# The small products of the recurrence's inverse, emitted in portions of sixteen columns of blocks

## The chip, the core and the metric

The kernel runs on one core of one Trainium2 chip. A core has a matrix engine (TensorE, PE in the profile, with its weight loads as PEld), three engines for element-wise work (VectorE or DVE, ScalarE or ACT, GpSimd or POOL) and a queue that issues transfers (SyncE, SP). Each engine takes its own instructions in order; between engines semaphores say when data is there. The metric is the device time of one execution in microseconds (us): less is better.

## What is computed

The reference is a two-layer encoder trunk for 256 positions of width 1024. Each layer has a token-mixing part and a channel mixer (dense in layer 0, eight experts in layer 1). Token mixing has two branches, which come out of one input projection and are merged by gates:

```python
for l in range(DEPTH):
    shift, scale, gate = ada_modulation(c, ada_w[l, 0], ada_b[l, 0])
    h = rmsnorm(x, norm_mix[l]) * (1.0 + scale) + shift
    proj = h @ w_in[l]
    ...
    y_a = rwkv7_branch(p_r, p_k, p_v, p_w, p_a, p_g, ...)
    y_b = mla_branch(q_a, kv_a, k_rope, cos, sin, ...)
    merged = jax.nn.sigmoid(g_a) * y_a + jax.nn.sigmoid(g_b) * y_b
    x = x + gate * (merged @ w_o[l])
```

The first branch is a recurrence over the positions, in each of eight heads, on a state of 64 x 64:

```python
def _rwkv7_step(state, inp):
    r, w, k, v, a, b = inp
    sa = jnp.einsum('bhvk,bhk->bhv', state, a)
    state = state * w[:, :, None, :] + sa[..., None] * b[:, :, None, :] + v[..., None] * k[:, :, None, :]
    y = jnp.einsum('bhvk,bhk->bhv', state, r)
    return state, y
```

The kernel computes it in chunks of 64 positions. Inside a chunk the effect of earlier positions on later ones is a triangular system, and its solution needs the inverse of a 64 x 64 triangular matrix for each head and chunk. That inverse is what the change is about.

## The kernel before

**Stages.** The kernel runs, one after the other: token mixing of layer 0 (`mix(0)`), a dense channel mixer (`ffn`), token mixing of layer 1 (`mix(1)`) and the experts (`moe`). A dense product is computed in three parts (L348, L349, L350 in `mm3`): activations and weights are each split into a high part in a faster number format and a remainder. The splits of the weights are an ACT copy (wh, L342) and a DVE subtraction (wl, L343) for each piece of 512 columns; `Stream.take` makes them up to four pieces ahead of use.

**What sets the order in token mixing.** `mix` merges four generators into one program. `dense` goes through a list: projections (a step is 12 products of 128 x 256), and between them products of the conditioning vector on DVE (`ada`, L383, 128 x 1024 each). Three chains run beside it: `rwkv` (the recurrence), `beside` (its side products) and `attend` (the second branch). Each `yield x` of a chain says how much dense work should pass before the chain's next piece: the chain becomes due at the present count plus x times a pace from the table `PACE`, and `mix` emits a chain's piece when it is due, and else a dense step (1.31 on this count for 12 products). A yield of any positive size therefore lets at least one dense step pass. At the entry `?y` of its list, `dense` waits until `rwkv` has reported "y"; `mix` then emits what is left of the recurrence without dense steps in between, and the output projection of the recurrence (`ro`, which reads yhi and ylo) comes next.

**The inverse.** The 64 x 64 triangle is inverted in blocks. DVE makes the inverses of 16 x 16 blocks (L1060 and on), and two levels of small products on PE put them together to 32 x 32 and to 64 x 64. At the first level four products of 32 x 32 stand side by side on the array, one for each of four places (p, d), and 16 columns of blocks (i = 0, 32, ..., 480) follow one another:
- Y0 (L1081, 64 products, the tile is called Y in the profile), then DVE adds the unit matrix and writes Ys (L1083, shown as f, Y, cst).
- M0T (L1090, 32 products) from Ys; DVE copies it (L1093).
- M0 (L1097, 64 products, tile M) from Ys; ACT copies it to AM in four pieces (L1100).
- The second level: Y1 (L1107, 32 products), and T21 (L1116, tile T, 32 products).

Each of these products is two matmul records and two weight loads in the profile (128 of each for Y0). Between the last `yield` of Y0 (1.2) and that of M0 nothing else is emitted on the chain: M0T and M0 follow one another at once.

**The end of the recurrence.** For each half of the positions, the products X, U, S and yps (L1139 to L1179) end in yps; then ACT squares it (ysq), DVE sums and takes a reciprocal root in small steps (yss, L358 to L364) and scales (yn, L1194); PE transposes (yT, L1199), DVE finishes (yo, L1202 and L1204), ACT and DVE split the result into yhi and ylo, which `ro` reads.

Of the kernel before, what the change touches and what calls it, by code (L numbers as in the profile page):

```python
# [322 lines left out]
class K:  # L323
# [571 lines left out]
    def rwkv(self, l):  # L895
# [183 lines left out]
        for i in range(0, 512, 32):  # L1079
            for p, d, q in blocks:  # L1080
                pe.matmul(ps[q:q + 32, i:i + 32], Uo[q:q + 32, i:i + 32], DT[q:q + 32, i:i + 32],  # L1081
                          start=True, stop=True, tile_position=(q, q))
        v.tensor_add(Ys.rearrange("p (c t) -> p c t", c=16), ps.rearrange("p (c t) -> p c t", c=16),  # L1083
                     self.c("eye32").unsqueeze(1).to_broadcast([128, 16, 32]))
        yield 1.2
# [5 lines left out]
                          start=True, stop=True, tile_position=(q, q))  # L1091
        for p, d, q in blocks[::2]:
            v.tensor_copy(DY[q:q + 32].rearrange("p h s -> p (h s)"), p2[q:q + 32])  # L1093
        ps = self.pr_("M0")
        for i in range(0, 512, 32):
            for p, d, q in blocks:
                pe.matmul(ps[q:q + 32, i:i + 32], Ys[q:q + 32, i:i + 32], Dd[q:q + 32, i:i + 32],  # L1097
                          start=True, stop=True, tile_position=(q, q))
        for p, d, q in blocks:
            act.activation(AM[q:q + 32, p, :, 0, 32 * d:32 * d + 32], ps[q:q + 32].rearrange("p (c t) -> p c t", c=16), AF.Copy)  # L1100
        yield 1.2
# [1075 lines left out]
```

## Time and profile before

| | us |
|---|---|
| median of three runs | 1722.49 |
| lowest and highest of the three | 1716.01, 1725.24 |
| profiled execution | 1726.71 |
| its span, first to last instruction | 1724.9 |
| PE busy | 1637.2 (95%) |
| DVE busy | 1458.6 (85%) |
| ACT busy | 1124.8 (65%) |

All times in the rows further down are microseconds from the start of the profiled execution's span. A row of the timeline has the start, the length, the engine, the line of the kernel, the operation with the tile it writes and those it reads, the shapes and how many records it joins; in brackets at its end stands how long the engine was idle before it and whose work ended that. The lengths of PE's records overlap, since products are pipelined: the pace of products is read from one start to the next.

### The profile page before, as it was taken

Reading aid. Unit: us, or ns where it says so; the run is one execution under the profiler, and the core shown is the slowest. Engines: PE = TensorE matmul, PEld = TensorE weight load, DVE = VectorE, ACT = ScalarE, POOL = GpSimd, SP = SyncE. Lnnn points to the kernel's source line nnn. Section 1 sums busy time; section 2 is a strip of 40 time slices with the busy share of each in tenths; the row PEclk is TensorE's granted clock in tenths of the full one; section 3 lists DMA queues with packets and bytes.
Section 4 is the critical chain, followed back from the end, with each engine's and each line's share of the span. In section 5 each row is a group of like instructions: output and inputs, shape, how many; then the busy total and the mean of one; then the engine's idle time right before and its main releaser. Section 6 shows DMA issues by size and latency. Waiting matters only on the chain.

```text
span 1724.9 us, 29083 instructions
## 1 busy us (share of the span) xinstructions
PE 1637.2 (95%) x10976; PEld 1415.8 (82%) x10976; DVE 1458.6 (85%) x2072; ACT 1124.8 (65%) x1481; POOL 6.6 (0%) x19
## 2 busy tenths in 40 slices
PE   4888999999989899989999999999999999999997
PEld 4877999999989789978877778867888678888885
DVE  6887678888868968769889988899898899888985
ACT  3655546555555545557768877778777688667774
POOL 0000000000000000000000000000000000000000
PEclk9998999999989989989999999999999999999998
DMA  8725466888733556778979999989999899999980
GB/s 272 267 91 163 156 192 213 279 294 292 258 110 114 163 169 202 266 311 319 364 293 367 420 420 378 341 329 420 419 418 344 330 380 419 420 370 357 352 342 27
DMA packets 92945, 501.94 MB, mean 291 GB/s; under 512 B 11498, under 2 KB 13034, under 8 KB 49788
## 3 DMA queue, kind: packets, MB, share of 16 engines
q1 hardware_dynamic: 91788, 498.54, 77.4%
q8 instruction: 88, 1.44, 0.3%
q10 hardware_dynamic: 720, 1.42, 0.3%
q14 instruction: 61, 0.50, 0.1%
q0 software_dynamic: 288, 0.03, 0.0%
HBM read 498.91 MB, written 1.05 MB: 290 GB/s over the span
## 4 chain that ended last, share of the span: by engine, by line
PE 83%; DVE 9%; issue 3%; ACT 2%; DMA 2%; DVEq 0%; ACTq 0%; SPq 0%
PE ph L349 7%; PE ph L350 7%; PE ph L348 7%; PE pj L348 6%; PE pj L349 5%; PE pj L350 5%; PE py L349 4%; PE py L350 4%; PE ph L1884 3%; PE ph L1883 3%; PE py L348 3%; DVE el L265 3%; PE psh L348 2%; PE psh L349 2%; PE psh L350 2%
## 5 line engine op out<-in xcount | busy, mean ns | idle before, releaser
L265 DVE TENSOR_TENSOR el<-er,eh 128x2048 fp32r<-128x2048 f32 (+1 forms) x268 | 585.8, 2220 | 25.6 <-ACT eh L259 14.7
L259 ACT ACTIVATE eh<-er 128x2048 fp32r<-128x2048 f32 (+1 forms) x268 | 491.1, 1862 | 50.5 <-PE ph L350 17.3
L342 ACT ACTIVATE wh<-wr 128x512 fp32r<-128x512 f32 (+1 forms) x366 | 223.5, 620 | 213.1 <-PE pj L349 65.4
L343 DVE TENSOR_TENSOR wl<-wr,wh 128x512 fp32r<-128x512 f32 (+1 forms) x366 | 243.1, 674 | 66.2 <-ACT wh L342 64.9
L348 PE MATMUL pj<-hhi,wh 128*128 128x256 f32 x704 | 210.0, 303 | 10.9 <-ACT hhi L468 9.9
L350 PE MATMUL pj<-hhi,wl 128*128 128x256 f32 x704 | 203.7, 291 | 0.6 <-DVE wl L343 0.6
L349 PE MATMUL pj<-hlo,wh 128*128 128x256 f32 x704 | 203.8, 291 | 0.1
L348 PEld LDWEIGHTS pj<-hhi,wh 128*128 128x128 f32 x704 | 137.0, 197 | 19.2 <-ACT hhi L468 11.1
L265 DVE TENSOR_TENSOR el<-x,eh 128x2048 fp32r<-128x2048 f32 x66 | 144.0, 2202 | 5.5 <-ACT eh L259 2.6
L349 PEld LDWEIGHTS pj<-hlo,wh 128*128 128x128 f32 x704 | 139.5, 198 | 2.9 <-issue 1.8
L350 PEld LDWEIGHTS pj<-hhi,wl 128*128 128x128 f32 x704 | 139.1, 198 | 1.6 <-DVE wl L343 0.8
L259 ACT ACTIVATE eh<-x 128x2048 fp32r<-128x2048 f32 x66 | 121.1, 1853 | 12.9 <-PE ph L350 5.4
L349 PE MATMUL py<-el,eahi 128*128 128x512 f32 x272 | 108.0, 397 | 3.4 <-DVE el L265 3.3
L350 PE MATMUL py<-eh,ealo 128*128 128x512 f32 x272 | 106.3, 391 | 0.0
L348 PE MATMUL py<-eh,eahi 128*128 128x512 f32 x272 | 101.5, 390 | 0.0
L349 PE MATMUL psh<-xu,wh 128*128 128x258 f32 x336 | 95.3, 284 | 0.0
L348 PE MATMUL psh<-xu,wh 128*128 128x258 f32 x336 | 95.2, 283 | 0.0
L350 PE MATMUL psh<-xu,wl 128*128 128x258 f32 x336 | 94.9, 282 | 0.0
L383 DVE SCALAR_TENSOR_TENSOR wr<-wr,cB 128x1024 f32<-128x1024 f32 x64 | 78.0, 1220 | 19.8 <-DMA wr<-in_ada_w_dram 19.6
L348 PE MATMUL ph<-eh,hhi 128*128 128x512 f32 x224 | 89.9, 404 | 0.0
L349 PE MATMUL ph<-el,hhi 128*128 128x512 f32 x224 | 89.0, 398 | 0.6 <-DVE el L265 0.6
L349 PE MATMUL ph<-el,hlo 128*128 128x512 f32 x224 | 88.6, 396 | 0.0
(469 smaller groups left out, 3642.8 us busy)
## 6 DMA issues: line engine op xcount, KB each, us to landing
er<-in_moe_w_dram SPq DMA_DIRECT2D x268, 1024.0 KB, 7.9
x<-in_moe_w_dram SPq DMA_DIRECT2D x66, 1024.0 KB, 7.6
wr<-in_ada_w_dram SPq DMA_DIRECT2D x64, 512.0 KB, 4.3
wr<-in_w_in_dram SPq DMA_DIRECT2D x52, 512.0 KB, 4.1
wr<-in_ffn_up_dram SPq DMA_DIRECT2D x44, 512.0 KB, 4.5
aw<-in_ada_w_dram SPq DMA_DIRECT2D x32, 512.0 KB, 4.8
wr<-in_ffn_w_dram SPq DMA_DIRECT2D x22, 512.0 KB, 4.5
wr<-in_w_o_dram SPq DMA_DIRECT2D x16, 512.0 KB, 4.3
```

The costliest lines, as they stand in the source:

```text
L259: self.k.tc.keep_in_program_order(nc.scalar.activation(t[4][:, :t[2]], t[3][:, :t[2]], AF.Copy))
L265: nc.vector.tensor_sub(t[5][:, :t[2]], t[3][:, :t[2]], t[4][:, :t[2]].bitcast(F32)))
L342: self.nc.scalar.activation(hi, src, AF.Copy)
L343: self.nc.vector.tensor_sub(lo, src, hi.bitcast(F32))
L348: mm(out, whi, xhi, start=start, stop=False, skip_group_check=True)
L349: mm(out, whi, xlo, start=False, stop=False, skip_group_check=True)
L350: mm(out, wlo, xhi, start=False, stop=stop, skip_group_check=True)
L383: x = v.scalar_tensor_tensor(w, w, 1.0, self.cB, op0=OP.mult, op1=OP.mult, accum_out=mod[:, n:n + 1])
L1883: pe.matmul(ps, x[0], w[0], start=start, stop=False, skip_group_check=True)
L1884: pe.matmul(ps, x[0], w[1], start=False, stop=stop, skip_group_check=True)
```

## The change

Seven `yield 0.1` are added to the recurrence's chain: after each of the first three quarters of Y0's products, between M0T's copies and M0, and after each of the first three quarters of M0's. What is computed, the number of instructions that compute it and their sizes stay as they are. The table `PACE` and the other yields are unchanged.

```diff
@@ -1080,6 +1080,8 @@
             for p, d, q in blocks:
                 pe.matmul(ps[q:q + 32, i:i + 32], Uo[q:q + 32, i:i + 32], DT[q:q + 32, i:i + 32],
                           start=True, stop=True, tile_position=(q, q))
+            if i % 128 == 96 and i < 480:
+                yield 0.1
         v.tensor_add(Ys.rearrange("p (c t) -> p c t", c=16), ps.rearrange("p (c t) -> p c t", c=16),
                      self.c("eye32").unsqueeze(1).to_broadcast([128, 16, 32]))
         yield 1.2
@@ -1091,11 +1093,14 @@
                           start=True, stop=True, tile_position=(q, q))
         for p, d, q in blocks[::2]:
             v.tensor_copy(DY[q:q + 32].rearrange("p h s -> p (h s)"), p2[q:q + 32])
+        yield 0.1
         ps = self.pr_("M0")
         for i in range(0, 512, 32):
             for p, d, q in blocks:
                 pe.matmul(ps[q:q + 32, i:i + 32], Ys[q:q + 32, i:i + 32], Dd[q:q + 32, i:i + 32],
                           start=True, stop=True, tile_position=(q, q))
+            if i % 128 == 96 and i < 480:
+                yield 0.1
         for p, d, q in blocks:
             act.activation(AM[q:q + 32, p, :, 0, 32 * d:32 * d + 32], ps[q:q + 32].rearrange("p (c t) -> p c t", c=16), AF.Copy)
         yield 1.2
```

After the edit a line number behind L1082 is greater by 2 to 5. The rows that follow are the order in which the two kernels give instructions to an engine, without times; rows of "..." leave out products that repeat the ones above them.

On PE, in layer 0, from Y0 (tile Y_1660) to M0, before; `pj<-` are the dense products, `sc` is the attention's:

```order
L1081 MATMUL Y_1660<-f_1262,f_1260 32x32 x64
L349 MATMUL pj<-hlo,wh 128x256
...
L1408 MATMUL sc<-kT_1640,qT_1642 128x128 x2
L1090 MATMUL M0T<-f_1263,f_1262 32x32 x32
L1097 MATMUL M_1788<-f_1262,f_1263 32x32 x64
```

and now, the same place:

```order
L1081 MATMUL Y_1660<-f_1262,f_1260 32x32 x16
L349 MATMUL pj<-hlo,wh 128x256
...
L1081 MATMUL Y_1660<-f_1262,f_1260 32x32 x16
L1413 MATMUL sc<-kT_1640,qT_1642 128x128 x2
...
L1432 MATMUL pT<-cst,e 128x128 x2
L1092 MATMUL M0T<-f_1263,f_1262 32x32 x32
...
L1100 MATMUL M_1894<-f_1262,f_1263 32x32 x16
L1413 MATMUL sc<-kT_1641,qT_1643 128x128 x2
```

Four portions of Y0 and four of M0 now stand where one of each stood. Between the first portion of Y0 and M0T there are 41 dense products in layer 0 (5 before) and 48 in layer 1 (17 before), and between the portions of M0 12 each.

On PE, at the end of the recurrence in layer 0: the last transposes yT and what follows them, before (the output projection, `pj<-yhi`, comes 60 dense products and three groups of the attention further on):

```order
L1437 MATMUL o<-eT,vv 64x128 x4
L1199 MATMUL yT<-cst,yn 128x128 x4
L348 MATMUL pj<-hhi,wh 128x256
L349 MATMUL pj<-hlo,wh 128x256
L350 MATMUL pj<-hhi,wl 128x256
```

and now:

```order
L350 MATMUL pj<-hhi,wl 128x256
L1204 MATMUL yT<-cst,yn 128x128 x4
L348 MATMUL pj<-yhi,wh 128x256 x2
L349 MATMUL pj<-ylo,wh 128x256
L350 MATMUL pj<-yhi,wl 128x256
```

The output projection has moved right behind yT; in layer 1 too, where 72 dense products stood between them. Between yps and yT stand 36 dense products in layer 0 (60 before) and 60 in layer 1 (60 before).

On DVE, the same end in layer 0, from the scaling yn to the split ylo, before:

```order
L1194 TENSOR_TENSOR yn<-yps,rs_y 128x512
...
L1202 SCALAR_TENSOR_TENSOR yo<-yT,prm,pv 128x128 x4
L343 TENSOR_TENSOR wl<-wr,wh 128x512
L1204 TENSOR_TENSOR yo<-yo,gate 128x4x128
L343 TENSOR_TENSOR wl<-wr,wh 128x512
L383 SCALAR_TENSOR_TENSOR wr,mod_1616<-wr,cB 128x1024
L343 TENSOR_TENSOR ylo<-yo,yhi 128x4x128
```

and now:

```order
L364 SCALAR_TENSOR_TENSOR rs_y<-rs_t,rs_y 128x8
L383 SCALAR_TENSOR_TENSOR wr,mod_1616<-wr,cB 128x1024
L1199 TENSOR_TENSOR yn<-yps,rs_y 128x512
L343 TENSOR_TENSOR wl<-wr,wh 128x512
L1207 SCALAR_TENSOR_TENSOR yo<-yT,prm,pv 128x128 x4
L1209 TENSOR_TENSOR yo<-yo,gate 128x4x128
L383 SCALAR_TENSOR_TENSOR wr,mod_1616<-wr,cB 128x1024
L343 TENSOR_TENSOR ylo<-yo,yhi 128x4x128
```

Two splits of weights (wl) have left the chain from yo to ylo, and a product of the conditioning (L383) has come in ahead of yn.

## Rows read from the trace of the kernel before

**Rows 1.** The page: busy time, share and instructions of each engine; the instruction queue.

```profile
PE 1637.2 (95%) x10976; PEld 1415.8 (82%) x10976; DVE 1458.6 (85%) x2072; ACT 1124.8 (65%) x1481; POOL 6.6 (0%) x19
...
q8 instruction: 88, 1.44, 0.3%
```

**Rows 2.** Stages: length; busy us of PE, PEld, DVE, ACT, POOL; clock; DMA; GB/s.

```profile
161.20:167.90 6.70, 6.69 (x116) 5.75 (x116) 2.13 (x5) 2.35 (x4) 0.00 (x0) 0.55 0.54 165
167.90:236.00 68.10, 67.82 (x798) 62.02 (x796) 49.64 (x133) 40.26 (x99) 0.00 (x0) 1.00 0.47 148
604.90:620.90 16.00, 14.87 (x206) 13.29 (x197) 6.35 (x11) 7.94 (x14) 0.00 (x0) 0.50 0.57 185
620.90:693.00 72.10, 71.59 (x756) 66.28 (x755) 59.27 (x155) 40.71 (x103) 0.00 (x0) 1.00 0.60 189
```

**Rows 3.** Timeline of PE in layer 0, M0T and M0.

```profile
154.95 0.66 PE L1090 MATMUL M0T<-f,f 32*32 32x32 f32 x29 [0.60 <-DVE f L1083]
155.84 0.69 PE L1090 MATMUL M0T<-f,f 32*32 32x32 f32 x32 [0.23 <-issue]
...
156.42 0.95 PE L1097 MATMUL M<-f,f 32*32 32x32 f32 x89
161.21 0.74 PE L1097 MATMUL M<-f,f 32*32 32x32 f32 x35 [3.83 <-issue]
```

**Rows 4.** Timeline of PE in layer 1: M0T, M0 and Y1.

```profile
602.43 1.16 PE L1090 MATMUL M0T<-f,f 32*32 32x32 f32 x61 [1.66 <-DVE f L1083]
...
603.46 1.60 PE L1097 MATMUL M<-f,f 32*32 32x32 f32 x126
...
607.98 1.92 PE L1107 MATMUL Y<-f,AM 32*32 32x32 f32 x64 [1.14 <-DVE wr L383]
```

**Rows 5.** Timeline of ACT in layer 1: the four copies of M0.

```profile
605.09 2.39 ACT L1100 ACTIVATE AM<-M 32x512 f32<-32x512 f32 x4 [1.33 <-PE M L1097]
```

**Rows 6.** Transfers from 150 to 170 us: packets, MB, share of 16 engines.

```profile
q8 instruction: 4, 0.07, 1.3%
```

**Rows 7.** Timeline of PE in layer 0: the last yps, and two dense products.

```profile
219.58 1.04 PE L1179 MATMUL yps<-Sb,AR 128*64 128x128 f32 x8
...
231.02 0.28 PE L349 MATMUL pj<-hlo,wh 128*128 128x256 f32 x1
231.14 0.28 PE L350 MATMUL pj<-hhi,wl 128*128 128x256 f32 x1
```

**Rows 8.** Timeline of DVE in layer 0, the end of the recurrence.

```profile
222.51 0.47 DVE L1419 TENSOR_SCALAR e<-e,rsum 128x128 f32<-128x128 f32 x2
...
225.61 0.68 DVE L1194 TENSOR_TENSOR yn<-yps,rs_y 128x512 f32<-128x512 f32 x1
...
231.20 1.12 DVE L1202 SCALAR_TENSOR_TENSOR yo<-yT,prm,pv 128x128 f32<-128x128 f32 x4
232.23 0.68 DVE L343 TENSOR_TENSOR wl<-wr,wh 128x512 fp32r<-128x512 f32 x1
232.83 0.68 DVE L1204 TENSOR_TENSOR yo<-yo,gate 128x512 f32<-128x512 f32 x1
...
234.03 1.22 DVE L383 SCALAR_TENSOR_TENSOR wr<-wr,cB 128x1024 f32<-128x1024 f32 x1
...
235.18 0.69 DVE L343 TENSOR_TENSOR ylo<-yo,yhi 128x512 fp32r<-128x512 f32 x1
```

**Rows 9.** Timeline of DVE in layer 1: Ys.

```profile
601.69 0.68 DVE L1083 TENSOR_TENSOR f<-Y,cst 128x512 f32<-128x512 f32 x1
```

**Rows 10.** Table of stages, at waits in layer 1.

```profile
565.00:569.00 4.00, 2.46 (x24) 2.36 (x25) 3.65 (x14) 2.26 (x7) 0.00 (x0) 1.00 0.45 131
569.00:573.00 4.00, 4.00 (x29) 3.69 (x28) 2.62 (x9) 1.28 (x4) 0.00 (x0) 0.62 0.55 148
584.00:588.00 4.00, 2.97 (x14) 2.09 (x13) 3.96 (x16) 1.76 (x5) 0.00 (x0) 1.00 0.51 140
588.00:592.00 4.00, 3.75 (x30) 3.30 (x29) 3.56 (x9) 3.17 (x8) 0.00 (x0) 1.00 0.39 128
```

## The prediction

> **What bounds the kernel now.** I read the page first: TensorE (PE) is busy 95% of the span [rows 1], so time can only come from the places where it stands still or runs slowly. The table of busy time and granted clock by stage then says which of these belong to the changed lines. From 161.2 to 167.9 us (layer 0) the granted clock is 0.55, nearly all of it at the lower level (1.2 GHz); from 604.9 to 620.9 us (layer 1) it is 0.50 throughout. In the stretches behind each, up to the end of the recurrence, it is 1.00 with PE busy in 67.8 of 68.1 and 71.6 of 72.1 us [rows 2]. So the rest of the mixing stage is bound by PE and whatever is saved ahead of it arrives at its end, unless something new waits there.
>
> The PE timeline shows how the dips begin. In layer 0 the product M0T waits 0.60 us for DVE (Ys), then runs, and M0 stops in its middle for 3.83 us with "issue" as the releaser: no data is awaited [rows 3]. In layer 1 M0T waits 1.66 us for Ys, and Y1 1.14 us (the profile names an unrelated DVE instruction; what Y1 really needs are ScalarE's four copies of M0, 2.39 us [rows 5], which start only when M0 has ended) [rows 4]. The clock is at the lower level after that pause, and after that run of small products with its waits.
>
> What is the pause? The instruction queue moved 88 blocks, 1.44 MB, in the whole run [rows 1], for 21952 PE instructions (10976 products, as many weight loads): about 250 instructions to a block. From 155.84 us to the pause, PE issues 128 small products with their weight loads (121 of them in the two rows, 7 in short rows between), that is 256 instructions in 1.5 us [rows 3]: one block. Four blocks came in the 20 us around it [rows 6], so a block per 5 us is what is seen when PE asks for the most, about 50 instructions per us. I take the pause for the wait for the next block.
>
> **The change part by part: what it gives.** No product is added or removed. Y0 and M0 (256 instructions each) now come in four portions of 64, and a dense step of 12 products stands between most of them: twelve at 0.12 us [rows 7], 1.4 us.
> 1. The pause. A portion and its step are 64 + 24 instructions, with the attention's products some 95, in about 0.3 + 1.4 + 0.4 = 2.1 us: 45 per us against the 50 seen. The pause should go: 3.83 + 0.23 us in layer 0. Whether a short one remains I cannot read from before: 0 to 1 us.
> 2. The waits of M0T. Ys is pushed back on DVE, since two attention steps and two products of the conditioning (L383, 1.15 us each [rows 8]) now stand ahead of it there; but PE has 41 dense products instead of 5 to do in between, 4.9 us. In layer 0 that about covers it: the 0.60 us goes. In layer 1 DVE comes late out of the rotary products (Ys could start at 601.69 us [rows 9]) and now has three splits (0.60 each) and two L383 ahead of Ys, 4.1 us: ready at 606.4 us. PE got to M0T at 602.43 - 1.66 = 600.8 us with 17 dense products behind Y0; with 48 it gets there 31 x 0.12 = 3.7 us later, and about 1.0 for three more breaks and a group of transposes: 605.5. So the 1.66 us becomes about 0.9. Y1's 1.14 us is covered by a dense step and three groups of transposes, 2.5 to 3 us, against the 2.39 us of copies: 0.3 left.
> 3. The clock. With a dense step after every 0.3 us of small products the mixture is like that of the later recurrence, which runs at 1.00 [rows 2]. Of the 6.7 us at 0.55 in layer 0, 0.45 x 6.7 = 3.0 come back; of the 14.87 busy us at 0.50 in layer 1, half: 7.4.
> Layer 0 gives 4.06 + 0.60 + 3.0 = 7.7, layer 1 0.8 + 0.8 + 7.4 = 9.0, together 16.7. Against it I set 1.3 us of new waits of dense products for their split weights: DVE has to make them in a time in which it was busy for only 2.13 of 6.7 and 6.35 of 16.0 us [rows 2], so it has the room, but not always in time (bounds 0 and 4). Gain: 15.4.
>
> **What it costs: the end of the recurrence.** Each of the seven new yields lets a dense step pass, so the recurrence ends seven steps later in the program, while the dense work ahead of "?y" stays the same. Before, 60 dense products stood behind the last yT in layer 0 and 72 in layer 1; now none do, and the first product of the output projection, which reads yhi and ylo, stands right behind yT in both. Nothing hides this chain any more.
> - From yT to ylo: in layer 0 DVE starts yo at 231.20 and ylo at 235.18 us [rows 8]. Two splits (0.60 each) that stood in the chain are gone in the new order, L383 is still there: 235.18 + 0.6 - 231.20 - 1.2 = 3.4 us. Two products that need only yhi (0.24) come earlier. PE idle: 3.2 us, in each layer.
> - Ahead of yT: from the end of yps (219.58 + 1.04) to the end of yn (225.61 + 0.68) before took 5.7 us [rows 7, 8]; the new order drops a softmax piece (0.47) and gains an L383 (1.15): 6.4 us. In layer 0 PE has only 36 dense products and one attention group for it, about 4.9 us: idle 1.5. In layer 1 it keeps 60 products and five groups, over 9 us: 0.
> - L383 stands ahead of both yn and ylo, and may wait for its weights; I add 0.5 us for each layer.
> Sum: 3.2 + 1.5 + 0.5 + 3.2 + 0.5 = 8.9 us.
> - The clock again. An idle PE loses it: with 2.46 us of work in 4.0 (1.54 idle), the next 4.0 us had 0.62 [rows 10]. The tails have less work than that, so I expect it in both layers. Price by that case: 0.38 of 4 us, that is 1.5 us; by layer 0's stretch behind M0, 3.0. I take 2.0 each: 4.0 us.
>
> Sum: -15.4 + 8.9 + 4.0 = -2.5 us. Against the profiled execution's own 1726.71 us that is 1724.2; it lies 4.2 us above the median of the three runs, 1722.49, so the forecast in terms of the median is 1720.0.
>
> **A rule that speaks against it.** The row shows 88 blocks of 16 KB on the instruction queue [rows 1]. The Trainium skill, "Runtime: NRT & Kernel Launch", section "Instruction fetch mechanics", says the same of the blocks (16 KiB, 256 instructions) and that the cost of crossing a block's boundary is mostly hidden. By that rule the 3.83 us would not be the fetch, and spreading the products would not remove it; the third rival below prices this from the rows.
>
> **The rivals.** First, **cheap tails**: no new waits on splits, no L383 that waits, and the clock keeps its level through the tails, because yT and the two early products cut the idle time into pieces. For it: 1.03 us of idle time in 4.0 elsewhere cost nothing in the clock [rows 10]; against it: the tails' pieces are longer. Then -16.7 + 7.9 = -8.8 us: 1713.7, and less where the lead that the splits win during the idle time saves a later wait. Chance 0.25.
> Second, **slower, by layer 1's dense steps starving**: Y0 ended at about 600.8 - 17 x 0.12 = 598.8 us, so PE wants its dense steps from there on, while DVE is in its rotary products until 601.69 us [rows 9]. If the dense products wait there for over some 2 us, PE is left with portions of 0.3 us and idle time, the clock falls as before, and now 36 more dense products lie in the slow stretch at 0.12 us more each, 4.3 us. Layer 1's gain turns to a loss of 4.3, layer 0 gives 7.7, the tails cost 12.9: +9.5 us, 1732.0. Against it: the splits are made up to four pieces ahead of their use. Chance 0.11.
> Third, **the portions don't remove the pause**, since it is not the fetch or comes at the next block. Layer 0 loses its 4.06 and 3.0 us: -2.5 + 7.1 = +4.6, 1727.1. Against it: layer 1 issues the same products (M0's 126 records run through in 1.60 us [rows 4]), so it is not the products themselves. Chance 0.11.
> The forecast has the rest, 0.53.
>
> **How the numbers follow.** Half a per cent, 8.6 us, is about what a measurement of this kernel can tell from no change. The forecast's own range is 1714 to 1727 (pause left over 0 to 1, splits 0 to 4, clock in the tails 0 to 6.0). It lies within the half per cent. Faster by over 0.5% (under 1713.9): 0.15 of the first rival and 0.06 of the forecast, 0.21. Slower (over 1731.1): 0.07 of the second and 0.05 of the others, 0.12. Same: 0.67. The range takes in the first rival and the third, and reaches just to the second's edge: 1711 to 1731.
>
> **What would show it.** Right: no "issue" pause in M0, M0T's wait in layer 1 near 1 us, the clock at 1.00 from 152 to 168 and 597 to 621 us; and, new, PE waiting for yo/yhi/ylo at the output projection's first products, 3 us in each layer, with a lower clock in the 4 us behind it. Wrong: a pause of several us that turns up in another small product; no idle time ahead of the output projection; or a clock of 0.5 among the portions of layer 1. The last would make the change slower, the absence of the tail faster than I say.

## The result: 0.6% slower

The median went from 1718.47 us (11 runs, 1714.19 to 1726.30) to 1729.23 us (11 runs, 1724.87 to 1740.34). The ratio is 1.0061, with a 95% interval of 1.0041 to 1.0080: 10.5 us slower (7.0 to 13.7). The forecast was 1720.0 with 0.12 for "slower by over 0.5%"; the time lies in its range of 1711 to 1731, but on the other side of no change.

The profiled execution after took 1734.05 us (span 1732.3), the one before 1726.71. Both lie above their medians, by 4.8 and 8.2 us, so the difference of the two spans is not the change's. I therefore also took one piece of equal work out of each trace: from the start of the 780th dense product (tile "pj") before the sum of squares "rms" that closes layer 0's mixing stage, up to that sum, and the same from the 800th in layer 1. These two pieces took 143.2 + 163.5 = 306.7 us before and 148.3 + 168.9 = 317.2 us after: 5.1 us more in layer 0 and 5.4 in layer 1. The rest of the program is the same within its own scatter.

The page of the changed kernel, busy time of PE:

```profile
PE 1637.1 (95%) x10976; PEld 1415.1 (82%) x10976; DVE 1461.2 (84%) x2072; ACT 1125.7 (65%) x1481; POOL 6.6 (0%) x19
```

The share is that of [rows 1]: nothing is to be seen there. The table of stages shows it (length; busy us of PE, PEld, DVE, ACT, POOL; granted clock; DMA share; GB/s), the changed kernel:

```profile
151.00:161.80 10.80, 8.66 (x180) 7.81 (x180) 8.74 (x20) 5.77 (x14) 0.00 (x0) 1.00 0.62 191
161.80:170.40 8.60, 8.60 (x169) 7.93 (x170) 7.23 (x15) 3.56 (x10) 0.00 (x0) 0.80 0.62 183
182.50:236.00 53.50, 53.03 (x636) 48.35 (x628) 36.96 (x103) 29.29 (x71) 0.00 (x0) 1.00 0.48 149
236.00:250.00 14.00, 8.23 (x41) 7.70 (x42) 7.51 (x15) 2.51 (x5) 0.00 (x0) 0.63 0.44 149
598.00:608.00 10.00, 8.38 (x181) 7.57 (x180) 8.89 (x16) 3.58 (x7) 0.00 (x0) 1.00 0.89 297
608.00:624.50 16.50, 14.71 (x335) 13.25 (x336) 12.85 (x29) 9.21 (x23) 0.00 (x0) 1.00 0.75 240
624.50:629.00 4.50, 4.50 (x80) 4.28 (x80) 2.18 (x5) 2.40 (x4) 0.00 (x0) 0.62 0.67 219
692.00:700.00 8.00, 6.81 (x31) 6.51 (x32) 4.47 (x9) 1.89 (x3) 0.00 (x0) 0.57 0.33 112
```

Compare with [rows 2]. The small products of layer 1 now run at a clock of 1.00 (598 to 624.5 us), as the change wanted it. But each layer has a dip among or behind the small products (161.8, 624.5) and a new one at the end of the recurrence (236, 692), where PE is busy for 8.23 of 14 and 6.81 of 8 us. Before, these ends stood at 1.00, with 13.27 of 14 us busy in layer 0 and no idle time in layer 1:

```profile
236.00:250.00 14.00, 13.27 (x115) 12.79 (x114) 9.70 (x19) 6.46 (x11) 0.00 (x0) 1.00 0.71 231
692.00:696.00 4.00, 4.00 (x37) 3.73 (x36) 3.12 (x7) 1.75 (x4) 0.00 (x0) 1.00 0.89 277
```

**The end of the recurrence.** The timeline of PE at the last yT and the first products of the output projection, layer 0 and then layer 1 (start, duration, line, tiles; in brackets the idle time before it and what ended it):

```profile
237.34 0.66 PE L1204 MATMUL yT<-cst,yn 128*128 128x128 f32 x4 [1.80 <-DVE yn L1199]
240.59 0.80 PE L348 MATMUL pj<-yhi,wh 128*128 128x256 f32 x2 [2.60 <-ACT yhi L342]
243.22 0.58 PE L349 MATMUL pj<-ylo,wh 128*128 128x256 f32 x1 [1.83 <-DVE ylo L343]
...
244.45 0.41 PE L348 MATMUL pj<-yhi,wh 128*128 128x256 f32 x1
244.66 0.41 PE L349 MATMUL pj<-ylo,wh 128*128 128x256 f32 x1
...
692.90 0.80 PE L348 MATMUL pj<-yhi,wh 128*128 128x256 f32 x2 [2.37 <-ACT yhi L342]
693.99 0.58 PE L349 MATMUL pj<-ylo,wh 128*128 128x256 f32 x1 [0.29 <-DVE ylo L343]
```

6.23 us idle in layer 0 and 2.66 in layer 1, and behind it dense products that start 0.21 us apart instead of 0.12 [rows 7]: 25 of them in layer 0 and 24 in layer 1, some 2.3 us each. Together 13.5 us. Of the last wait in layer 0, the 1.83 us for ylo, most is a conditioning product (L383) ahead of ylo on DVE, which waited 1.45 us for its own weight:

```profile
241.32 1.23 DVE L383 SCALAR_TENSOR_TENSOR wr<-wr,cB 128x1024 f32<-128x1024 f32 x1 [1.45 <-DMA wr<-in_ada_w_dram]
```

**Behind the small products.** Layer 0, PE and then ACT, and the queue that loads the weights (SPq):

```profile
161.78 0.64 PE L1398 MATMUL qkT<-cst,q 128*96 128x128 f32 x4 [2.12 <-ACT e L1420]
...
166.93 0.52 PE L1100 MATMUL M<-f,f 32*32 32x32 f32 x32
...
169.43 0.45 PE L1100 MATMUL M<-f,f 32*32 32x32 f32 x32
```

```profile
160.19 0.63 ACT L342 ACTIVATE wh<-wr 128x512 fp32r<-128x512 f32 x1 [2.45 <-DMA wr<-in_w_in_dram]
160.73 0.46 ACT L1420 ACTIVATE e<-sc,mx 128x256 f32<-128x256 f32 x1
```

```profile
146.47 0.33 SPq L171 DMA_DIRECT2D wr<-in_ada_w_dram  x1
152.97 1.81 SPq L171 DMA_DIRECT2D wr<-in_w_in_dram  x2
```

and the same place before, ACT and the queue:

```profile
157.51 0.63 ACT L342 ACTIVATE wh<-wr 128x512 fp32r<-128x512 f32 x1 [2.97 <-DMA wr<-in_w_in_dram]
```

```profile
147.29 0.33 SPq L171 DMA_DIRECT2D wr<-in_ada_w_dram  x1
153.78 2.08 SPq L171 DMA_DIRECT2D wr<-in_w_in_dram  x2
```

The portions of M0 run without the "issue" pause of [rows 3]. But PE now waits 2.12 us for the exponentials "e" of the attention. They stand in ScalarE's queue behind a weight's split, and that waits 2.45 us for its weight, one of the two loads issued from 152.97 us on; the queue had issued nothing since 146.47 us. The gap in the loads is not new: before it lay between 147.29 and 153.78 us, and ScalarE waited 2.97 us for a weight behind it. What is new is that PE comes to the work behind that split before the weight is there. In layer 1, PE and then DVE:

```profile
608.06 1.20 PE L1092 MATMUL M0T<-f,f 32*32 32x32 f32 x64 [1.67 <-DVE f L1085]
...
620.28 0.64 PE L1398 MATMUL qkT<-cst,q 128*96 128x128 f32 x4 [0.64 <-ACT e L1420]
...
622.85 0.44 PE L1432 MATMUL pT<-cst,e 128*128 128x128 f32 x2 [1.10 <-DVE kT L1404]
```

```profile
606.16 1.23 DVE L383 SCALAR_TENSOR_TENSOR wr<-wr,cB 128x1024 f32<-128x1024 f32 x1 [0.67 <-DMA wr<-in_ada_w_dram]
...
607.32 0.69 DVE L1085 TENSOR_TENSOR f<-Y,cst 128x512 f32<-128x512 f32 x1
```

M0T waits as long as before [rows 4], now because a product of the conditioning, itself late by 0.67 us for its weight, stands ahead of Ys on DVE; and two products of the attention wait for 0.64 and 1.10 us.

**What a portion costs by itself.** PE in layer 1, a dense product, a portion of M0, and the dense products behind it:

```profile
610.59 0.28 PE L350 MATMUL pj<-hhi,wl 128*128 128x256 f32 x1
610.79 0.45 PE L1100 MATMUL M<-f,f 32*32 32x32 f32 x32
611.18 0.38 PE L348 MATMUL pj<-hhi,wh 128*128 128x256 f32 x1
611.40 0.28 PE L349 MATMUL pj<-hlo,wh 128*128 128x256 f32 x1
611.52 0.28 PE L350 MATMUL pj<-hhi,wl 128*128 128x256 f32 x1
```

Starts of dense products lie 0.12 us apart; from the last one to the portion it is 0.20, from the first one behind the portion to the next 0.22. A break therefore costs some 0.18 us, and seven more of them 1.3 us in each layer.

### The profile page after: what moved, and what is told of

Its sections match the earlier page's. It is cut to its first block, busy times and chain, and to the rows that moved or that the text cites. A ratio compares the mean times of both kernels' runs of the same rounds, so it can differ in the third digit from the quotient of the medians.

```text
span 1732.3 us, 29087 instructions
## 1 busy us (share of the span) xinstructions
PE 1637.1 (95%) x10976; PEld 1415.1 (82%) x10976; DVE 1461.2 (84%) x2072; ACT 1125.7 (65%) x1481; POOL 6.6 (0%) x19
## 4 chain that ended last, share of the span: by engine, by line
PE 80%; DVE 10%; DMA 4%; issue 2%; ACT 2%; DVEq 0%; ACTq 0%; SPq 0%
PE ph L349 7%; PE ph L350 7%; PE ph L348 7%; PE pj L348 5%; PE pj L349 5%; PE pj L350 5%; PE py L349 4%; PE ph L1889 3%; PE py L350 3%; PE ph L1888 3%; PE py L348 3%; DVE el L265 3%; PE psh L348 2%; PE psh L349 2%; PE psh L350 2%
## 5 line engine op out<-in xcount | busy, mean ns | idle before, releaser
L383 DVE SCALAR_TENSOR_TENSOR wr<-wr,cB 128x1024 f32<-128x1024 f32 x64 | 78.0, 1222 | 16.9 <-DMA wr<-in_ada_w_dram 16.6
```

Of the source, the lines that this page charges most:

```text
L383: x = v.scalar_tensor_tensor(w, w, 1.0, self.cB, op0=OP.mult, op1=OP.mult, accum_out=mod[:, n:n + 1])
```

## The experiments

Twelve runs, in which a "step" is a dense step of 12 products that is let past, so that the recurrence ends one step later. The column of the mixing stages is the equal work of the section above, from one trace each; us are worked out from the ratio and the median of before (1717 to 1721 us) beside it.

| kernel | steps | ratio to before (95%) | us | mixing stages, us |
|---|---|---|---|---|
| before | 0 | 1 | 0 | 306.7 |
| changed | 7 | 1.0061 (1.0041 to 1.0080) | +10.5 | 317.2 |
| late_seven | 7 | 1.0082 (1.0062 to 1.0102) | +14.1 | 320.8 |
| after_mo_first | 7 | 1.0012 (0.9999 to 1.0026) | +2.1 | 303.0 |
| late_seven_mo | 7 | 1.0017 (1.0001 to 1.0033) | +2.9 | 309.0 |
| before_mo_first | 0 | 1.0002 (0.9987 to 1.0016) | +0.3 | 306.6 |
| m0_two_halves | 1 | 0.9993 (0.9979 to 1.0006) | -1.2 | 300.7 |
| m0_two_halves_again | 1 | 1.0011 (0.9995 to 1.0028) | +1.9 | 307.2 |
| y0_portions_only | 3 | 0.9981 (0.9965 to 0.9996) | -3.3 | 302.3 |
| m0_portions_only | 4 | 0.9963 (0.9948 to 0.9979) | -6.4 | 298.2 |
| m0_portions_mo_first | 4 | 0.9950 (0.9927 to 0.9973) | -8.6 | 297.9 |
| halves_both | 2 | 0.9931 (0.9908 to 0.9954) | -11.9 | 295.5 |
| halves_again | 2 | 0.9935 (0.9912 to 0.9958) | -11.2 | 295.0 |
| halves_mo_first | 2 | 0.9938 (0.9913 to 0.9964) | -10.7 | 292.6 |

Theory A: the loss is the wait at the recurrence's output projection, because the recurrence ends seven steps later. Theory B: the portions themselves cost.

**The delay alone.** late_seven is the kernel before with

```
+        for _ in range(7):
+            yield 0.1
         ps = self.pr_("Y0")
```

> The kernel before, with no portions, but seven dense steps let past ahead of Y0 in one piece, so that the recurrence ends as late as in the changed kernel. Theory A: the tails' cost without the portions' saving: 11 to 16 us above before, idle time of 5 to 6 us and a lower clock at the recurrence's projection in layer 0, 2 to 3 us idle in layer 1. Theory B: within 3 us of before.

Measured: 14.1 us above before (10.7 to 17.5). Its list of PE's waits in layer 0 (us in total, times, longest):

```profile
PE M L1099 <- issue: 4.2, 1, 4.2
PE pj L348 <- ACT yhi L342: 2.6, 1, 2.6
PE pj L349 <- DVE ylo L343: 2.1, 1, 2.1
PE pT L1429 <- ACT e L1417: 2.0, 1, 2.0
PE yT L1201 <- DVE yn L1196: 1.8, 1, 1.8
```

The same three waits at the end as in the changed kernel, without any portion: B, which wanted it within 3 us of before, cannot be the whole. The pause in M0 is there as well (4.2 us), and so is a wait of 2.0 us for "e", without portions and ahead of the pause. The delay also moves the inverse itself: in layer 1 its lower clock lasts from 624.3 to 631.1 us only, where before it stood at 0.50 from 604.9 to 620.9 us [rows 2]. So the 14.1 us are not the tail alone.

**The tail taken away.** after_mo_first and before_mo_first exchange the output projections, which puts the attention's 96 dense products behind the last yT:

```
-        body += ["?y"] + each([f"ro{c}" for c in range(4)])
         body += ["?o"] + each([f"mo{c}" for c in range(4)])
+        body += ["?y"] + each([f"ro{c}" for c in range(4)])
```

> The changed kernel with the two output projections of each layer in the other order (attention's first, the recurrence's second), so that 96 dense products lie behind the last yT. Theory A (the loss is the wait of the recurrence's output projection: in the changed kernel 6.2 us idle and 3.2 us at the lower clock in layer 0, 2.7 and 3.1 us in layer 1, 15.2 together): no idle time over 0.5 us ahead of either projection, clock 1.0 there, and 3 to 5 us below the kernel before (13 to 15 below the changed kernel). Theory B (the portions themselves cost, by breaks in the dense work and new waits on the engines beside; the end of the recurrence only shows a wait that would come elsewhere): within 3 us of the changed kernel, so 7 to 10 us above before.

> The kernel before with the same exchange of the two projections and nothing else. Theory A: nothing to gain, because no wait stood ahead of the recurrence's projection: 0 in layer 0, and in layer 1, where the last product of the attention came 2 us after the projection's start, 0 to 3 us slower. If this alone gains 3 us or more, the exchange has a merit of its own and its run on the changed kernel does not speak for theory A.

Measured: 2.1 us above before (0.2 below to 4.5 above), and for the control 0.3 (2.2 below to 2.7 above). The two tails of after_mo_first in the table of stages:

```profile
236.00:250.00 14.00, 14.00 (x122) 14.00 (x121) 13.79 (x28) 6.61 (x12) 0.00 (x0) 1.00 0.79 249
682.00:690.00 8.00, 8.00 (x69) 7.66 (x69) 7.39 (x16) 3.85 (x9) 0.00 (x0) 1.00 0.58 192
```

PE is full and the clock at 1.00 where the changed kernel had 8.23 of 14 us and 0.63. So the tail is what made the change slower: without it 8.4 us are back, and the exchange has no merit of its own. But both theories are off on the rest. A wanted a gain of 3 to 5 us over before to remain, since the portions were to save something; by the medians none is seen: 2.1 us against 0.3 for the control, with intervals that overlap. By the single traces 3.6 us are seen (303.0 against 306.6).

**What the portions save.** late_seven_mo is late_seven with the same exchange.

> The seven dense steps ahead of Y0 in one piece and no portions, with the attention's output projection ahead of the recurrence's, so that nothing waits at the end of the recurrence. Against the changed kernel with the same exchange (1719.4, 2 us above before) only the portions are missing, so the difference is what the portions themselves save. Theory A (from the two runs with the tail, 1732.7 against 1729.2): they save 3 to 4 us: 4 to 7 us above before. If they save what the prediction's sum said, 15 us: 17 above. If nothing: 2 above.

Measured: 2.9 us above before (0.2 to 5.7), that is 0.9 us above after_mo_first. A saving of 15 us, which would have put it at 17, is excluded. By the traces the difference is 6.0 us (309.0 against 303.0), but the two intervals overlap and a single trace does not carry a few us (next experiment): from nothing to some 6 us is what can be said. It is also a saving over an inverse that the delay had already changed: here, too, the lower clock of layer 1's inverse is left from 617.2 to 620.7 us only, without any portion. What tests the sum's gain of 15.4 is after_mo_first against before_mo_first.

**One yield in M0.** m0_two_halves is the kernel before with

```
                           start=True, stop=True, tile_position=(q, q))
+            if i == 224:
+                yield 0.1
```

in M0 alone.

> The kernel before with one yield in the middle of M0 and no other, one dense step of delay against the 60 and 72 dense products in hand behind the last yT. If the 3.83 us pause in M0 of layer 0 is the fetch of the next block of instructions and one dense step covers it, it is gone: 3 to 5 us below before, or 6 to 7 if the clock behind it comes back too. If the pause only moves to another place among the small products: within 2 us of before.

> M0 alone in two halves, measured again, because its first median (1 us below before) and its trace disagree: there the two mixing stages together are 6 us shorter than in the kernel before (300.7 against 306.7 us), as those of Y0 and M0 in halves are 11 us shorter, which its medians bear out. If the trace is right: 4 to 8 us below before. If the first median is right, the second half, that of Y0, is worth 10 us: 0 to 2 below.

Measured: 1.2 us below before (3.6 below to 1.0 above) and 1.9 above (0.9 below to 4.8 above): no difference, and the 4 to 8 us that the first trace promised are not there. The second halves of M0 in layer 0, of the first and of the second trace:

```profile
156.03 0.61 PE L1097 MATMUL M<-f,f 32*32 32x32 f32 x47 [0.62 <-issue]
```

```profile
157.56 0.64 PE L1097 MATMUL M<-f,f 32*32 32x32 f32 x47 [2.19 <-issue]
```

One step in its middle shortens the pause from 3.83 us [rows 3], to 0.62 in one execution and 2.19 in another, and does not remove it. In layer 1 both traces have a new "issue" pause ahead of a dense product (1.32 and 1.92 us), where the kernel before waited 1.14 us at Y1 [rows 4]. So the pause moves, as the second reading has it. The mixing stages of the two traces differ by 6.5 us, nearly all of it in layer 1 (161.0 and 167.2): a single trace of this kernel does not carry a few us.

**Portions in Y0 or in M0 alone.**

> Portions in Y0 alone: three steps of delay. Theory A with a threshold: in the kernel before, layer 0 had 3.9 us in hand between ylo (235.8) and the first product of the output projection (239.7), 2.7 steps of 1.45 us, and layer 1 some 8.7 us, 6 steps; the three steps cost 0.5 us in layer 0 and nothing in layer 1, the pause in M0 stays: 1 us below to 2 above before. Rival without a threshold (each step costs its share of 14 us in seven): 5 to 6 above.

> Portions in M0 and the yield behind M0T alone: four steps of delay. Theory A with the threshold: layer 0 is over by 1.3 steps, 1.9 us idle and 1 to 3 us at the lower clock, layer 1 by nothing; the pause in M0 is gone, of which some 1 to 3 us arrive: 1 us below to 3 above before. Rival without a threshold: 6 to 8 above, less the pause.

Measured: 3.3 us below before (0.7 to 6.0), and 6.4 below (3.6 to 8.9). Both are better than either expectation. The rival without a threshold falls: three and four steps cost nothing like their share of 14 us. The first products of the projection in layer 0, of y0_portions_only and then m0_portions_only:

```profile
239.06 0.39 PE L348 MATMUL pj<-yhi,wh 128*128 128x256 f32 x1 [0.20 <-ACT gb L764]
240.31 0.39 PE L349 MATMUL pj<-ylo,wh 128*128 128x256 f32 x1 [0.86 <-DVE ylo L343]
```

```profile
233.43 0.50 PE L348 MATMUL pj<-yhi,wh 128*128 128x256 f32 x2 [1.67 <-ACT yhi L342]
235.12 0.39 PE L349 MATMUL pj<-ylo,wh 128*128 128x256 f32 x1 [1.19 <-DVE ylo L343]
```

1.06 us idle at three steps, 2.86 at four, 6.23 (with the wait ahead of yT) at seven; in layer 1 neither has a wait there. With one step of 1.45 us and 2.7 steps in hand in layer 0, a straight line gives 0.4, 1.9 and 6.2. In layer 0 the threshold is there; it is softer than the line. The two traces also tell the other costs apart. PE in y0_portions_only, layer 0 and layer 1:

```profile
165.49 0.64 PE L1395 MATMUL qkT<-cst,q 128*96 128x128 f32 x4 [1.94 <-ACT e L1417]
```

```profile
609.87 0.64 PE L1099 MATMUL M<-f,f 32*32 32x32 f32 x30 [3.60 <-issue]
```

The wait for the late weight by way of "e" comes with the portions of Y0 (1.94 us; 0.63 with those of M0), or rather with the dense steps let past ahead of M0T: late_seven has it without portions. And the pause, which the kernel before had only in layer 0, stands here in layer 1 and not in layer 0: it is no property of one product.

**Two halves each.** halves_both has the yield of m0_two_halves in Y0 and in M0.

> Y0 and M0 in two halves each, one yield in the middle of each: two steps of delay, within what both layers have in hand. Theory A: no wait at the output projection, no pause in M0: 1 to 4 us below before. Rival without a threshold: 2 to 4 above, less the pause.

> The kernel with Y0 and M0 in two halves each, measured again beside before, because its gain of 0.7% came out three times as large as expected. Theory A (threshold at the end of the recurrence, pause gone in layer 0): 6 to 13 us below before if the gain is real; 1 to 4 below if the first measurement was a lucky one.

Measured: 11.9 us below before (7.9 to 15.8), and on another chip 11.2 (7.2 to 15.1); the medians alone are 8.6 and 10.3 us apart. The gain is real; it is far over the 1 to 4 us that I gave it first. Stages of halves_again, both inverses (the kernel before has 0.79 from 151.8 to 168 and 0.77 from 597.2 to 610 us), and its list of PE's waits in layer 0:

```profile
151.30:165.50 14.20, 13.54 (x444) 12.12 (x444) 13.58 (x30) 9.25 (x21) 0.00 (x0) 1.00 0.59 188
585.70:600.70 15.00, 12.18 (x439) 11.18 (x438) 12.35 (x22) 6.57 (x12) 0.00 (x0) 1.00 0.86 278
```

```profile
PE qkT L1397 <- DVE q L1378: 1.0, 1, 1.0
PE pj L349 <- DVE ylo L343: 0.4, 1, 0.4
...
PE M L1099 <- issue: 0.3, 1, 0.3
PE Y L1111 <- issue: 0.3, 1, 0.3
```

The pause is down to 0.3 us, no wait for "e" has come in its place, the clock stays at 1.00 in both inverses, and 0.4 us is all that waits at the projection. In layer 1 a pause of 1.91 us is left in the middle of M0. Of the 11.2 us by the traces (306.7 against halves_both's 295.5), 8.2 are in layer 0.

**The exchange where little waits.**

> The two halves with the attention's output projection ahead of the recurrence's. Theory A: the two steps of delay lie within what is in hand, only 0.4 us was idle at the output projection, so the exchange has nothing to take away: within 3 us of the halves alone. If the end of the recurrence still costs something that the idle time does not show: 3 us or more below them.

> Portions in M0 and the yield behind M0T, with the attention's output projection first. Theory A: four steps are over the threshold of layer 0, where 2.9 us were idle at the output projection; they go, so 2 to 5 us below the same kernel without the exchange, 8 to 12 below before. If the end of the recurrence does not matter at four steps: within 1 us of it.

Measured: 10.7 us below before (6.2 to 15.0), the same as the halves without it; and 8.6 below (4.6 to 12.6), 2.2 under m0_portions_only. The exchange is worth 0 at two steps, some 2 at four, 8 to 11 at seven: as theory A has it, though at four steps the two intervals overlap.

What the runs leave open: why seven steps without a tail (after_mo_first) lie 12.8 us above two (halves_mo_first). Their traces differ by 5.6 us in layer 0 and 4.9 in layer 1. Read from them: in layer 0 a wait of 1.93 us for "e", a clock of 0.77 from 157 to 172 us behind it, and five more breaks of 0.18; in layer 1 waits of 2.05 us ahead of M0T, 0.89 and 0.40 for the attention, and 1.26 in the recurrence, where halves_mo_first has 0.61 ahead of M0T, a pause of 0.90 in M0 and 0.19 for the attention. That the late weights are the cause in layer 0 is argued from the order of ScalarE's queue and was not tried by itself; what the runs show is that the wait is there with three or seven dense steps ahead of M0T, with portions or without, and not with one.

## Why the prediction was wrong, step by step

The sum was -15.4 for the inverse, +8.9 for idle tails, +4.0 for the clock in them: -2.5. The runs put +2.1 in the place of the first term (after_mo_first) and +8.4 in the place of the other two (changed against after_mo_first): +10.5. **The step that failed is the gain of 15.4.** Its mechanisms came, but the new waits that it allowed for (1.3 us), the clock that it counted on in layer 1 (7.4 us) and the breaks that it put at nothing were mis-sized; items 2 to 5 have what they measured.

1. The pause. Right: it is gone from M0 in layer 0, and no other small product has it. Most of the 4.06 us is taken up by a new wait: with three dense steps let past ahead of M0T, PE comes to the gap in the loads earlier and waits 2.12 us for "e", with the clock down for 12 dense products and a portion behind it (some 1.2 us). The removed pause does not bring this wait: late_seven has both, and halves_both neither, and its layer 0 is 8.2 us shorter.
2. The waits ahead of M0T. Layer 0: gone, as forecast. Layer 1: 1.67 instead of 0.9; I had counted the work ahead of Ys on DVE (4.1 us) but not that L383 would wait for its own weight, 0.67. Y1's own wait is gone, but 0.64 and 1.10 stand ahead of it at the attention's products.
3. The clock. The mechanism was right in layer 1: 1.00 all through the small products. Its size was too large. Half of 14.87 us was to come back; at the lower level a dense product takes 0.21 us against 0.12, Y1's 64 took 1.92 [rows 4] against 1.20 after. With 32 dense products in that stretch at 0.09 each, 0.7 us each for Y1 and T, and 1.3 for X, U and the attention's qkT, some 5.6 of the 7.4 us were there to be had. And two new dips, behind the new waits, took part of it back: in layer 0 that of item 1, in layer 1 another 12 dense products, some 1.1 us.
4. The 1.3 us for new waits of dense products (bounds 0 and 4). This is the term that was mis-sized most. I asked whether DVE could make the split weights in time; what was late was the weight itself, on ScalarE's queue, and the attention's work stood behind it. Waits and the dips behind them come to 3.3 us in layer 0, and 1.7 us of waits alone in layer 1.
5. The breaks between small and dense products were costed at nothing. They take 0.18 us each, 2.5 us in all. With 0.8 us from item 2, 1.8 and 1.1 from item 3 and 3.7 from item 4 (3.3 + 1.7, less the 1.3 allowed), some 10 of the 15.4 us are accounted for. The rest, a gain of some 5 us, is near the 3.6 us of the single traces with the exchange (303.0 against 306.6), while their medians show none; that difference stays open.
6. The tails. Idle 6.23 us in layer 0 and 2.66 in layer 1, against 3.2 + 1.5 + 0.5 and 3.2 + 0.5: 8.9 forecast, 8.9 in the trace. That the sum fits is luck: layer 0 is 1.0 us over, mostly because L383 waited 1.45 us for its weight where 0.5 was set, and layer 1 is 1.0 under. The clock behind them, 4.0 forecast, is some 4.6. With the traces' 13.5 us against the forecast's 12.9, the mechanism and its size hold; late_seven's 14.1 agrees, though its delay changed more than the tail. By the exchange only 8.4 come back, in part since the recurrence's projection, now last, makes its own consumers wait (two of 0.7 us at the merged halves in layer 0); the rest of that difference is open.

The rivals. "Cheap tails" falls. "Slower by layer 1's dense steps starving" had the right side for the wrong reason: from 598 to 608 us, where it wanted waits and a low clock, the clock is 1.00. "The portions don't remove the pause" falls for the changed kernel.

What the pause is. Where small products follow each other for long, there are pauses of 3.83 us before, 4.2 in late_seven, 3.60 in y0_portions_only, 0.3 and 1.91 with two halves; there is none over 0.5 us with M0 in four portions, where dense products lie between every 64 of its instructions (the changed kernel, m0_portions_only and both with the exchange). The traces say more: they have the times of the packets on the instruction queue (q8, [rows 1]). Before, one ended at 159.86 us, and PE went on at 161.21, 1.35 us later. The same holds for every "issue" pause of PE of over 0.5 us in the mixing stages of all fourteen traces, 20 pauses in ten of them: each ends 1.2 to 1.5 us behind the end of a block's packet. That the pause is the wait for the next block, as the prediction took it, is what this timing shows; no run changed the fetch itself. The Trainium skill, "Runtime: NRT & Kernel Launch", section "Instruction fetch mechanics", says that the cost of crossing a block's boundary is mostly hidden. The traces agree with that for the portions, and not for the long runs of small products. One reading of the prediction is put in doubt by the same times: Y1's 1.14 us before [rows 4] also ended 1.50 us behind a packet's end (606.48 us), and 0.50 behind the copies that the prediction named, so it may have been a wait for a block too.

The base was too high as well: the three runs shown had a median of 1722.49, eleven have 1718.47. From there the same sum would have given 1716.

The version that beats both is halves_both: 1711.97 and 1710.32 us, 0.7% under before by the ratios in the table.

## What to carry to other kernels

Before work is let in between, count how many steps the chain that is pushed back has in hand at its far end, here 2.7 steps in layer 0; up to that a delay was nearly free there (0.4 us idle at two steps), and beyond it the steps are paid, with the clock on top (6.23 us idle at seven). Work that is let past early also asks for its inputs early: three or seven dense steps ahead of M0T met a weight that was not there yet and cost 1.9 to 2.1 us, one did not. So look up when the loads land before adding steps. And try the smallest number of cuts first: two gave 11 us, seven took 10.

## What the runs showed that I had not expected

The pause for no data moves. It is 3.83 us in layer 0 and none in M0 of layer 1 before, 3.60 in layer 1 and nothing in layer 0 with portions in Y0, and 0.62 or 2.19 in two executions of one kernel. And executions of one kernel scatter with the granted clock: the changed kernel took 1724.87 us at a mean clock of 0.982 and 1740.34 at 0.973, so one profile is no measure of half a per cent.
